# Gate and up in seven products: the seventh product's weight sum on VectorE, and products weight tile by weight tile with the high parts first

## The chip, the cores and the metric

The kernel runs on one core of a Trainium2 chip. The metric is device microseconds of one execution of the whole program: 1477.72 us is the median of three runs (1474.51 to 1479.86). Engines are named as in the profile: PE is TensorE (PEld its weight loads), DVE is VectorE, ACT is ScalarE, POOL is GpSimd, SP is SyncE, which here only issues DMAs.

## The reference, cut to what matters

A trunk of two layers over 512 tokens of 1024 features, in float32. Layer 0 mixes tokens by dilated window attention, layer 1 by gated linear attention; after each comes a feed-forward part:

```
def swiglu(h, w_gate_up, w_down):          # hidden width 2816
    g, u = jnp.split(h @ w_gate_up, 2, axis=-1)
    return (jax.nn.silu(g) * u) @ w_down

    h = h + mix.astype(h.dtype)
    h = h + swiglu(rms_norm(h, ffn_norm[i]), ffn_w_gate_up[i], ffn_w_down[i]).astype(h.dtype)
```

The change lies in the product `h @ w_gate_up` of both layers (512 x 1024 by 1024 x 5632).

## The kernel before, in words

**Split products.** Every float32 operand is split in two: ACT rounds it to the matmul's format (the high part, tiles `wh`), DVE subtracts that from the original (the low part, `wl`). A product is then three matmuls: high by high, high by low, low by high. `split` (lines 92 to 98) does it for weights: line 96 on ACT, line 97 on DVE. There are three buffers for `wh` and three for `wl`, each of 128 x 1024.

**Seven products for eight.** Gate and up are computed as a block product of 2 x 2 blocks: the tokens in two halves, the features in two halves, gate and up as the two column blocks. A scheme of Strassen's kind (Winograd's form) needs seven block products instead of eight, at the price of sums of blocks. The sums of the activations (`S1` to `S4`, made by `pair_sums` and `last_sums`, tiles `sh` and `sl`) are made once in a layer; the sums of the weights are made for every group of columns anew. The 2816 columns go in six groups `j`: five of 512, the last of 256. In each group the products come in the order first, second, fifth, sixth, third, seventh, fourth. One product is 24 matmuls of 128 x 512 (4 feature tiles, 2 token tiles, 3 terms), into two PSUM banks of 512 columns, one per token tile `i`. First, sixth, seventh and fourth add into the same pair of banks (`ppp`), and ACT copies the running sum out (line 379, tiles `g`) after the first, sixth and seventh; fifth and third share another pair (`ps`).

**The weights.** `forms` (line 236) is a generator: each step yields the split tiles of the next product. A 512-column block is two tiles of 128 x 1024 ("tile 1" and "tile 2" here; a tile holds two feature tiles). In groups 1 to 4 (`own` is false) the steps are:

- first: plain load of block 0 into `wA`, split
- second: plain load of block 1 into `wf`, split
- fifth: a DMA from POOL adds block 2 into `wA` in memory (line 251, `accum_op`), split; block 3 is loaded into `wB`
- sixth: DVE adds `wB` to `wA` (line 296), split
- third: a DMA adds block 1 into `wA`; `wB` as it stands is split
- seventh: a DMA adds block 2 into `wB`, split
- fourth: `wA` is split

Groups 0 and 5 (`own`) load a second copy of block 3 and make their sums ahead. `wf` has two buffers, `wB` two, `wA` four; `wf` also carries all plain weights of the other parts of the kernel.

**The order of the work.** Python issues the operations in program order; a scheduler with priorities (`high_priority` lets the steps of `forms` run ahead, `issue_after` holds something back) then writes one list per engine. Every engine works its list in order. What stands on DVE and ACT between the splits is the rest of the group: gates (lines 392, 393), the sums of lines 420, 421, 430 and 445, copies (379) and transposes (351). Finished columns go to memory by POOL's DMAs (`put`, line 359, held back until the last accumulating DMA of the group is issued) and come back transposed through SP's (`get`, line 365).

**The products.** `product` (lines 317 to 330) walks feature tile by feature tile; for each token tile it issues `xh` by `wh` (328), `xh` by `wl` (329) and `xl` by `wh` (330).

Of the kernel before, what the change touches and what calls it, by code (L numbers as in the profile page):

```python
# [21 lines left out]
P = 128  # L22
D = 1024
S = 512
KT = D // P
# [14 lines left out]
class Trunk:  # L40
# [195 lines left out]
    def forms(self, dram, own, ahead=0):  # L236
        nc = self.nc
        n = dram.shape[1]
        raw = {}
        started = ahead  # L240

        def load(block, tag, at=None, queue=nc.sync):
            raw[tag] = []
            for i in range(n):
                w = self.t(at or tag, (P, 1024))
                queue.dma_start(w, dram[block, i])
                raw[tag].append(w)

        def add(tag, block):
            for i in range(n):  # L250
                self.added = nc.gpsimd.dma_start(raw[tag][i], dram[block, i], accum_op=ALU.add)  # L251

        def ready(tag):
            return [self.split(w, (P, 1024), "wh", "wl") for w in raw[tag]]

        def sums(queue=nc.sync):
            load(0, "wA", queue=queue)
            add("wA", 2)
            load(3, "wB", queue=queue)
            raw["wC"] = raw["wB"]  # L260
            if not started:
                other_sum()

        def other_sum(queue=nc.sync):
            load(3, "wB", "wA", queue=queue)
            add("wB", 2)

        def first():
            if own and ahead:
                with self.tc.high_priority(offset=OUT):  # L270
                    sums(nc.gpsimd)
            if not own:
                load(0, "wA")
                return ready("wA")
            load(0, "wf")
            return ready("wf")

        def second():
            if own and not started:
                with self.tc.issue_after(self.added.ins):  # L280
                    sums()
            load(1, "wf")
            return ready("wf")

        def fifth():
            if not own:
                add("wA", 2)
                load(3, "wB")
                raw["wC"] = raw["wB"]
            elif started:  # L290
                other_sum(nc.gpsimd)
            return ready("wA")

        def sixth():
            for i in range(n):
                nc.vector.tensor_add(raw["wA"][i], raw["wA"][i], raw["wC"][i])
            return ready("wA")

        def third():
            add("wA", 1)  # L300
            return ready("wC")

        def seventh():
            if not own:
                add("wB", 2)
            return ready("wB")

        def fourth():
            return ready("wA")

        for step in (first, second, fifth, sixth, third, seventh, fourth):
            with self.tc.high_priority(offset=AHEAD + ahead):
                w = step()
            ahead = 0
            yield w

    def product(self, acc, x, w, width, start):
        mm = self.nc.tensor.matmul
        per = 1024 // width
        last = KT // 2 - 1  # L320
        for k in range(KT // 2):
            wh, wl = w[k // per]
            f = slice(k % per * width, (k % per + 1) * width)
            xh, xl = x[k]
            for i in range(2):
                tok = slice(i * P, (i + 1) * P)
                a = acc[i][:, 0:width]
                mm(a, lhsT=xh[:, tok], rhs=wh[:, f], start=start and k == 0, stop=False, skip_group_check=True)  # L328
                mm(a, lhsT=xh[:, tok], rhs=wl[:, f], start=False, stop=False, skip_group_check=True)  # L329
                self.multiplied = mm(a, lhsT=xl[:, tok], rhs=wh[:, f], start=False, stop=k == last, skip_group_check=True)  # L330

    def gate_up(self, layer, acts):
        nc = self.nc
# [915 lines left out]
```

## Time and profile before

| | |
|---|---|
| median of three runs | 1477.72 us (1474.51 to 1479.86) |
| span of the profiled execution, first to last instruction | 1475.3 us |
| time of that execution beside its span | not given by the page; the three runs are others |
| PE busy | 1449.8 us, 98% |
| DVE, ACT, POOL busy | 992.6, 756.1, 162.7 us |
| gate and up of layer 0, of layer 1 | about 565 to 787 us, 1128 to 1354 us |
| of these, groups 1 to 4 | about 604 to 762 us, 1167 to 1329 us |
| accumulating DMAs into `wB`, groups 1 to 4 | 8 in each layer |
| granted TensorE clock | 0.998 |

In a row of the timeline stand start, duration, engine, line, operation, and in brackets the idle time before it with what ended it. In the list of waits: engine, tile and line that waited, what it waited for, microseconds in total, how often, and the longest. In a grouped row: busy time and mean ns, then the idle time and its parts. A row of a window has busy time and count of PE, PEld, DVE, ACT and POOL, then the clock, the DMA engines' share and GB/s.

### The profile page before, as it was taken

The numbers are of one execution on the slowest core, as the hardware profiler recorded it, in microseconds if no ns is written. First come the engines' busy times: TensorE is split into PE (matmuls) and PEld (weight loads), VectorE is DVE, ScalarE is ACT, GpSimd is POOL, SyncE is SP. The second block draws the span as 40 slices with busy tenths as digits, with TensorE's granted clock in tenths as the row PEclk, the third lists the DMA queues.
The fourth block names the chain that finished last, engine by engine and source line by source line (L and its number), as shares of the span: only waits on it lengthen the run. The fifth ranks groups of instructions, "written<-read, shape, count | busy, mean of one in ns | idle before, by whom it ended". The sixth has DMA issues, their size and how long they took to land.

```text
span 1475.3 us, 20977 instructions
## 1 busy us (share of the span) xinstructions
PE 1449.8 (98%) x7742; PEld 1184.5 (80%) x7742; DVE 992.6 (67%) x1808; ACT 756.1 (51%) x1292; POOL 162.7 (11%) x272
## 2 busy tenths in 40 slices
PE   8999999999999999999999999999999999999998
PEld 6877878787778888877787887888888777778887
DVE  6586868778678669877676435756667876669322
ACT  6344444545566747655565324555745755556221
POOL 0001020101100021122230000000010122221000
PEclk9999999999999999999999999999999999999999
DMA  8644443454433365788887333212264788788431
GB/s 275 183 134 109 104 123 108 109 180 93 131 94 101 87 190 154 195 218 214 220 222 210 95 101 103 86 45 84 71 189 125 229 215 208 208 182 250 143 104 61
DMA packets 99831, 219.61 MB, mean 149 GB/s; under 512 B 15216, under 2 KB 42416, under 8 KB 99728
## 3 DMA queue, kind: packets, MB, share of 16 engines
q1 hardware_dynamic: 81072, 158.35, 34.5%
q0 software_dynamic: 18656, 59.91, 19.1%
q8 instruction: 61, 1.00, 0.3%
q14 instruction: 42, 0.34, 0.1%
HBM read 185.64 MB, written 19.99 MB: 139 GB/s over the span
## 4 chain that ended last, share of the span: by engine, by line
PE 66%; DVE 10%; issue 10%; DMA 7%; ACT 5%; POOL 1%; SPq 1%; DVEq 0%; POOLq 0%; ACTq 0%
PE ppp L110 9%; PE ppp L109 9%; PE ppp L108 9%; PE ppp L570 6%; PE ppp L571 6%; PE ppp L572 6%; PE ppp L329 3%; PE ppp L328 3%; PE ppp L330 3%; DVE wl L97 3%; DMA wA<-in_gate_up_last_dram 2%; DMA wB<-in_gate_up_dram 2%; PE po L701 2%; ACT wh L96 1%; PE ps L661 1%
## 5 line engine op out<-in xcount | busy, mean ns | idle before, releaser
L96 ACT ACTIVATE wh<-wf 128x1024 fp32r<-128x1024 f32 (+1 forms) x184 | 191.4, 1041 | 317.6 <-PE ppp L109 174.6
L97 DVE TENSOR_TENSOR wl<-wf,wh 128x1024 fp32r<-128x1024 f32 (+1 forms) x184 | 219.9, 1196 | 187.1 <-ACT wh L96 186.6
L570 PE MATMUL ppp<-wh,xs 128*128 128x512 f32 (+1 forms) x672 | 258.2, 385 | 7.2 <-ACT wh L96 5.7
L571 PE MATMUL ppp<-wl,xs 128*128 128x512 f32 (+1 forms) x672 | 257.3, 383 | 0.1
L572 PE MATMUL ppp<-wh,xs 128*128 128x512 f32 (+1 forms) x672 | 257.0, 383 | 0.0
L570 PEld LDWEIGHTS ppp<-wh,xs 128*128 128x128 f32 x672 | 126.8, 189 | 36.4 <-ACT wh L96 5.7
L572 PEld LDWEIGHTS ppp<-wh,xs 128*128 128x128 f32 x672 | 126.8, 189 | 25.6 <-issue 1.2
L571 PEld LDWEIGHTS ppp<-wl,xs 128*128 128x128 f32 x672 | 127.1, 189 | 24.8 <-DVE wl L97 0.9
L96 ACT ACTIVATE wh<-wA 128x1024 fp32r<-128x1024 f32 x88 | 93.2, 1059 | 73.4 <-PE ppp L330 27.3
L97 DVE TENSOR_TENSOR wl<-wA,wh 128x1024 fp32r<-128x1024 f32 x88 | 107.4, 1220 | 22.4 <-ACT wh L96 22.2
L329 PE MATMUL ppp<-wl,a 128*128 128x512 f32 (+1 forms) x288 | 108.1, 375 | 1.0 <-DVE wl L97 0.5
L328 PE MATMUL ppp<-wh,a 128*128 128x512 f32 (+1 forms) x288 | 108.4, 377 | 0.1
L108 PE MATMUL ppp<-xs,wh 128*128 128x512 f32 x272 | 106.5, 392 | 0.0
L109 PE MATMUL ppp<-xs,wh 128*128 128x512 f32 x272 | 106.5, 393 | 0.0
L110 PE MATMUL ppp<-xs,wl 128*128 128x512 f32 x272 | 106.0, 391 | 0.0
L330 PE MATMUL ppp<-wh,a 128*128 128x512 f32 (+1 forms) x288 | 105.5, 372 | 0.0
L97 DVE TENSOR_TENSOR wl<-wB,wh 128x1024 fp32r<-128x1024 f32 x38 | 46.5, 1223 | 78.2 <-ACT wh L96 78.2
L649 ACT ACTIVATE sm<-sm,st 128x160 f32<-128x160 f32 (+2 forms) x128 | 56.9, 446 | 43.5 <-DVE st L648 43.4
L329 PE MATMUL ppp<-wl,sh 128*128 128x512 f32 (+1 forms) x192 | 72.8, 379 | 4.6 <-DVE wl L97 4.4
L328 PE MATMUL ppp<-wh,sh 128*128 128x512 f32 (+1 forms) x192 | 71.9, 375 | 2.5 <-ACT g L379 1.8
L330 PE MATMUL ppp<-wh,sl 128*128 128x512 f32 (+1 forms) x192 | 71.6, 373 | 0.0
L251 POOL DMA_DIRECT2D wA<-in_gate_up_dram x44 | 38.5, 874 | 298.9 <-DVE wl L97 210.1
(319 smaller groups left out, 2949.0 us busy)
## 6 DMA issues: line engine op xcount, KB each, us to landing
wA<-in_gate_up_dram POOLq DMA_DIRECT2D x52, 512.0 KB, 6.1
wf<-in_down_dram SPq DMA_DIRECT2D x32, 512.0 KB, 3.7
wf<-in_gate_up_dram SPq DMA_DIRECT2D x24, 512.0 KB, 5.0
wf<-in_a_w_v_dram SPq DMA_DIRECT2D x20, 512.0 KB, 3.8
wB<-in_gate_up_dram POOLq DMA_DIRECT2D x20, 512.0 KB, 6.4
turned<-g POOLq DMA_DIRECT2D x80, 128.0 KB, 6.3
wf<-in_a_w_q_dram SPq DMA_DIRECT2D x16, 512.0 KB, 3.9
zq<-zs SPq DMA_DIRECT2D x128, 64.0 KB, 2.1
```

What stands on the lines that cost most here:

```text
L96: nc.scalar.activation(hi, src, AF.Copy)
L97: self.low = nc.vector.tensor_sub(lo, src, hi.bitcast(F32))
L108: mm(out, lhsT=wh, rhs=xh, start=start, stop=False)
L109: mm(out, lhsT=wh, rhs=xl, start=False, stop=False)
L110: self.multiplied = mm(out, lhsT=wl, rhs=xh, start=False, stop=stop)
L328: mm(a, lhsT=xh[:, tok], rhs=wh[:, f], start=start and k == 0, stop=False, skip_group_check=True)
L329: mm(a, lhsT=xh[:, tok], rhs=wl[:, f], start=False, stop=False, skip_group_check=True)
L330: self.multiplied = mm(a, lhsT=xl[:, tok], rhs=wh[:, f], start=False, stop=k == last, skip_group_check=True)
L570: mm(a, lhsT=xh, rhs=wh[:, f], start=k == 0, stop=False)
L571: mm(a, lhsT=xh, rhs=wl[:, f], start=False, stop=False)
L572: self.multiplied = mm(a, lhsT=xl, rhs=wh[:, f], start=False, stop=k == KT - 1)
L649: nc.scalar.activation(sm[:, w], sm[:, w], AF.Exp, bias=n, scale=-1.0, accum_out=l)
```

## The change

Two edits. In groups 1 to 4, block 2 is loaded a second time, plainly, into `wf` (issued by SP in the sixth step's place), and DVE adds `wB` (named `wC`) to it; the accumulating DMA into `wB` is gone. And `product` now goes weight tile by weight tile: first all matmuls that need the high part of the tile, then those that need its low part; in all but the last tile of a product for both token tiles together, in the last tile for token tile 0 completely and then for token tile 1.

```diff
         def sixth():
+            if not own:
+                load(2, "wf")
             for i in range(n):
                 nc.vector.tensor_add(raw["wA"][i], raw["wA"][i], raw["wC"][i])
             return ready("wA")
...
         def seventh():
-            if not own:
-                add("wB", 2)
-            return ready("wB")
+            if own:
+                return ready("wB")
+            for i in range(n):
+                nc.vector.tensor_add(raw["wf"][i], raw["wf"][i], raw["wC"][i])
+            return ready("wf")
...
-        for k in range(KT // 2):
-            wh, wl = w[k // per]
+        def high(i, k, wh):
             f = slice(k % per * width, (k % per + 1) * width)
-            xh, xl = x[k]
-            for i in range(2):
-                tok = slice(i * P, (i + 1) * P)
-                a = acc[i][:, 0:width]
-                mm(a, lhsT=xh[:, tok], rhs=wh[:, f], start=start and k == 0, stop=False, skip_group_check=True)
-                mm(a, lhsT=xh[:, tok], rhs=wl[:, f], start=False, stop=False, skip_group_check=True)
-                self.multiplied = mm(a, lhsT=xl[:, tok], rhs=wh[:, f], start=False, stop=k == last, skip_group_check=True)
+            for x_part, first in zip(x[k], (start and k == 0, False)):
+                mm(acc[i][:, 0:width], lhsT=x_part[:, i * P:(i + 1) * P], rhs=wh[:, f], start=first, stop=False,
+                   skip_group_check=True)
+
+        def low(i, k, wl):
+            f = slice(k % per * width, (k % per + 1) * width)
+            self.multiplied = mm(acc[i][:, 0:width], lhsT=x[k][0][:, i * P:(i + 1) * P], rhs=wl[:, f], start=False,
+                                 stop=k == last, skip_group_check=True)
+
+        for n, (wh, wl) in enumerate(w):
+            ks = range(n * per, n * per + per)
+            for group in ((0, 1),) if n < len(w) - 1 else ((0,), (1,)):
+                for i in group:
+                    for k in ks:
+                        high(i, k, wh)
+                for i in group:
+                    for k in ks:
+                        low(i, k, wl)
```

Lines from 331 on are 14 higher in the changed kernel; below, 309 is the new addition, 328 the matmuls on high parts and 333 those on low parts.

How the lists of the engines move is shown at three places. The first is DVE at the fifth and sixth products of group 2, layer 0; a row gives line, operation, output and inputs with buffer numbers. Before:

```order
L97 TENSOR_TENSOR wl_6639<-wf_6632,wh_6638 128x1024
L351 STREAM_TRANSPOSE g_6580<-g_6529 128x2x8x32
L97 TENSOR_TENSOR wl_6681<-wA_6587,wh_6680 128x1024
L296 TENSOR_TENSOR wA_6587<-wA_6587,wB_6676 128x1024
L97 TENSOR_TENSOR wl_6685<-wA_6589,wh_6684 128x1024
L392 TENSOR_TENSOR g_6625<-ppp_6628,g_6625 128x512
L296 TENSOR_TENSOR wA_6589<-wA_6589,wB_6678 128x1024
L97 TENSOR_TENSOR wl_6720<-wA_6587,wh_6719 128x1024
```

and now:

```order
L97 TENSOR_TENSOR wl_6643<-wf_6636,wh_6642 128x1024
L365 STREAM_TRANSPOSE g_6584<-g_6533 128x2x8x32
L309 TENSOR_TENSOR wf_6721<-wf_6721,wB_6680 128x1024
L97 TENSOR_TENSOR wl_6685<-wA_6591,wh_6684 128x1024
L298 TENSOR_TENSOR wA_6591<-wA_6591,wB_6680 128x1024
L97 TENSOR_TENSOR wl_6689<-wA_6593,wh_6688 128x1024
L309 TENSOR_TENSOR wf_6723<-wf_6723,wB_6682 128x1024
L298 TENSOR_TENSOR wA_6593<-wA_6593,wB_6682 128x1024
L97 TENSOR_TENSOR wl_6728<-wA_6591,wh_6727 128x1024
```

The additions for the seventh product stand three products ahead of it: the first ahead of the fifth product's first low part, the second ahead of the sixth product's sum. `wf_6721` is loaded into the buffer that the second product's split frees. (In group 1 both stand later, among the sixth product's low parts.)

The second place is PE where the seventh product of group 2 gives way to the fourth. Before, the fourth begins:

```order
L328 MATMUL ppp_6585<-wh_6833,a_5738 128x512
L329 MATMUL ppp_6585<-wl_6834,a_5738 128x512
L330 MATMUL ppp_6585<-wh_6833,a_5739 128x512
L328 MATMUL ppp_6585<-wh_6833,a_5789 128x512
L329 MATMUL ppp_6585<-wl_6834,a_5789 128x512
```

and now, with the last rows of the seventh (operands `sh`, `sl`) ahead of it:

```order
L328 MATMUL ppp_6590<-wh_6808,sl_5914 128x512
L333 MATMUL ppp_6590<-wl_6809,sh_5862 128x512
L333 MATMUL ppp_6590<-wl_6809,sh_5913 128x512
L328 MATMUL ppp_6589<-wh_6841,a_5738 128x512
L328 MATMUL ppp_6589<-wh_6841,a_5739 128x512
L328 MATMUL ppp_6589<-wh_6841,a_5789 128x512
L328 MATMUL ppp_6589<-wh_6841,a_5790 128x512
L333 MATMUL ppp_6589<-wl_6842,a_5738 128x512
L333 MATMUL ppp_6589<-wl_6842,a_5789 128x512
L328 MATMUL ppp_6590<-wh_6841,a_5738 128x512
```

The bank of token tile 0 (`ppp_6589`) gets its last matmul of the seventh product six matmuls before the end of it, where it was three, and the bank of token tile 1 is first written six matmuls into the fourth.

The third place is ACT in group 0 of layer 1, at the copies (line 379 before, 393 now) after the seventh product. Before:

```order
L379 ACTIVATE g_10714<-ppp_10438 128x512
L96 ACTIVATE wh_10776<-wA_10772 128x1024
L114 ACT_TABLE_LOAD
L114 ACTIVATE Rc_10627<-Rc_10626 128x4
L379 ACTIVATE g_10714<-ppp_10439 128x512
L115 ACT_TABLE_LOAD
L115 ACTIVATE Rc_10627<-Rc_10627 128x4
```

and now:

```order
L393 ACTIVATE g_10730<-ppp_10454 128x512
L114 ACT_TABLE_LOAD
L114 ACTIVATE Rc_10643<-Rc_10642 128x4
L96 ACTIVATE wh_10792<-wA_10788 128x1024
L115 ACT_TABLE_LOAD
L115 ACTIVATE Rc_10643<-Rc_10643 128x4
L393 ACTIVATE g_10730<-ppp_10455 128x512
```

The second copy moved behind the second table load. On POOL the two accumulating DMAs of each group are gone from between the third product's and the finished columns' writes; SP's list has the new loads behind the next group's first weights.

## The prediction

> **What bounds the kernel now.** The page's first part came first, then the waits of TensorE's weight loads, then single stretches in order of time.
>
> ```profile
> span 1475.3 us, 20977 instructions
> PE 1449.8 (98%) x7742; PEld 1184.5 (80%) x7742; DVE 992.6 (67%) x1808; ACT 756.1 (51%) x1292; POOL 162.7 (11%) x272
> ```
>
> TensorE (PE) is busy 98% of the span, so nothing outside its own stream matters unless PE is kept waiting. But ends of matmuls are modelled, so I read starts. The timeline at the seventh product of column group 3, layer 0:
>
> ```profile
> 709.26 0.39 PE L329 MATMUL ps<-wl,sh 128*128 128x512 f32 x1
> 709.49 0.39 PE L330 MATMUL ps<-wh,sl 128*128 128x512 f32 x1
> 709.77 0.51 PE L328 MATMUL ppp<-wh,sh 128*128 128x512 f32 x1
> 711.03 0.50 PE L329 MATMUL ppp<-wl,sh 128*128 128x512 f32 x1 [0.75 <-DVE wl L97]
> ```
>
> Undisturbed, starts are 0.227 us apart; a product of 24 takes 5.45. Here 711.03 - 709.77 = 1.26: one matmul with a low weight part lost 1.03 us. How much of this there is in the whole run stands in the waits of the weight loads (PEld; total us, times, longest). These rows belong to the gate and up products alone:
>
> ```profile
> PEld ppp L329 <- DVE wl L97: 13.9, 22, 1.1
> PEld ppp L328 <- ACT g L379: 6.9, 14, 1.5
> PEld ppp L328 <- ACT wh L96: 2.1, 4, 0.9
> ```
>
> Together 22.9 us in 40 waits. A load always idles a little (0.227 - 0.188 = 0.04 us, load time below), so 21.3 us is all that can be lost there, and the most that the change can win. By form:
>
> ```profile
> L329 PEld LDWEIGHTS ppp<-wl,a 128*128 128x128 f32 x288 | 54.2, 188 | 13.5 <-DVE wl L97 4.5
> L329 PEld LDWEIGHTS ppp<-wl,sh 128*128 128x128 f32 x192 | 36.1, 188 | 15.3 <-DVE wl L97 9.3
> ```
>
> 9.3 us stand before seventh products (sh), 4.5 in fourth and first ones (a), behind the same delay. Its origin in group 2:
>
> ```profile
> 662.57 0.89 POOL L251 DMA_DIRECT2D wB<-in_gate_up_dram  x1 [1.86 <-DVE wl L97]
> 668.83 1.06 ACT L96 ACTIVATE wh<-wB 128x1024 fp32r<-128x1024 f32 x1 [2.89 <-DMA wB<-in_gate_up_dram]
> 671.32 1.06 ACT L96 ACTIVATE wh<-wB 128x1024 fp32r<-128x1024 f32 x1 [1.43 <-DMA wB<-in_gate_up_dram]
> ```
>
> The accumulating DMA may start only when the third product's split has read wB; its 6.2 us are too long, and ScalarE (ACT) idles for it.
>
> **The change part by part.**
>
> *Sum on VectorE.* Both operands of the seventh sum are now loaded a product or more earlier, so the 6.2 us leave the path. VectorE (DVE) gets 16 additions of the size of
>
> ```profile
> L296 DVE TENSOR_TENSOR wA<-wA,wB 128x1024 f32<-128x1024 f32 x22 | 26.7, 1213 | 0.3
> 604.00:762.00 158.00, 156.22 (x674) 125.06 (x673) 112.43 (x126) 91.00 (x113) 40.61 (x57) 1.00 0.83 204
> ```
>
> 16 x 1.213 = 19.4 us. In groups 1 to 4 of layer 0 (second row) DVE is busy 112.4 of 158 us; with 8 more it is 122. As a load it is covered; what counts is where the additions stand. In groups 2 to 4 the first stands behind the second product's low parts, and its operand is loaded into the buffer that those have just freed:
>
> ```profile
> 646.05 3.32 SPq L246 DMA_DIRECT2D wf<-in_gate_up_dram  x2
> DMA to landing us min/median/max: 4.7/5.9/6.9
> 648.93 0.70 DVE L351 STREAM_TRANSPOSE g<-g 128x512 f32<-128x512 f32 x1
> 650.12 1.23 DVE L97 TENSOR_TENSOR wl<-wA,wh 128x1024 fp32r<-128x1024 f32 x1 [0.48 <-ACT wh L96]
> 654.26 0.39 PE L328 MATMUL ps<-wh,sh 128*128 128x512 f32 x1
> 659.71 0.39 PE L328 MATMUL ppp<-wh,sh 128*128 128x512 f32 x1
> ```
>
> (The second row is of these wf loads.) DVE reaches the addition at 649.6 and stands until 646.05 + 5.9 = 652.0, at worst 653.0. Behind it waits everything on DVE; PE feels the low parts of the fifth product (start 654.26) and the sixth (659.71). At worst: addition 654.2, fifth's first low part 655.4, sum and second low part 657.8, addition and sum 660.2, sixth's first low part 661.5, gate addition and second low part 663.4. They are wanted at 656.1, 657.9, 661.5 and 663.3, since the new order wants the first low part of a tile after 8 matmuls (1.82 us), of a last tile after 4 (0.91). So at 6.9 it just fits, at 5.9 with 1 us to spare; each us beyond 6.9 costs one us in six places (three groups, two layers). Below zero it cannot be: no earlier work depends on it. I take 0.2 each, 1.2 us; bounds 0 and, at the longest landing of a like load (9.4, quoted below), 6 x 2.5 = 15.
>
> The Trainium skill has a rule against this part (PSUM — Partial Sum Buffer, section Engine vs sequencer instructions): VectorE's queue is strictly first in, first out, so that ready splits cannot pass a waiting addition. By it the sum has the 1.2 us, up to 15; could they pass, 0. The trace shows nothing that speaks against it: DVE idles at 650.12 for its next instruction's operand.
>
> *Queues.* POOL loses 16 issues (0.89 us at 662.57) and its writes of the finished group move up by as much; nobody waits for them sooner. SP gets 16 plain loads. Behind them stand its loads for the next group: those of wf, that before followed the second product's low parts, now follow the seventh's, which leaves them the fourth and first products, 10.9 us, against at most 6.9. Cost 0; without that cover, what lands later than 10.9.
>
> *High parts first.* Low parts are wanted 8 or 4 matmuls into a tile, before after 1. That alone covers waits up to 1.59 or 0.68 us; with the DMA gone I remove 13.4 of the 13.9 us and all of the 2.1 for wh. The copies (6.9 us, 14): at the fourth product PE writes a bank that ACT is still copying.
>
> ```profile
> 676.32 0.39 PE L330 MATMUL ppp<-wh,sl 128*128 128x512 f32 x1
> 676.71 0.50 PE L328 MATMUL ppp<-wh,a 128*128 128x512 f32 x1
> 676.06 0.60 ACT L379 ACTIVATE g<-ppp 128x512 f32<-128x512 f32 x1 [0.98 <-PE ppp L330]
> 677.71 0.58 ACT L379 ACTIVATE g<-ppp 128x512 f32<-128x512 f32 x1
> ```
>
> The first copy starts 0.26 us before the last matmul, because its bank got its last one only 3 before the end. Now it is 6: the copy ends about 0.5 us before the product does. The second, behind a split of 1.06, ends 1.2 us after the product, and its bank is wanted after 6 matmuls (1.36). Where the 6.9 us lie: groups 1 to 4 (first row, the same in each layer), group 5 of layer 0 and of layer 1:
>
> ```profile
> PEld ppp L328 <- ACT g L379: 1.7, 4, 0.4
> PEld ppp L328 <- ACT g L379: 1.9, 2, 1.5
> PEld ppp L328 <- ACT g L379: 1.0, 2, 0.6
> ```
>
> Of 3.4 us in groups 1 to 4 I remove 2.8 and leave 0.6 for the narrow margin (1.36 against 1.2). In group 5 the second copy stands behind a split that waits for a DMA:
>
> ```profile
> 776.85 1.06 ACT L96 ACTIVATE wh<-wA 128x1024 fp32r<-128x1024 f32 x1 [2.10 <-DMA wA<-in_gate_up_last_dram]
> 777.81 0.37 ACT L379 ACTIVATE g<-ppp 128x256 f32<-128x256 f32 x1
> 778.23 0.19 PEld L328 LDWEIGHTS ppp<-wh,sh 128*128 128x128 f32 x1 [1.54 <-ACT g L379]
> ```
>
> PE now has 12 matmuls for the other bank instead of 3, each half as wide and so about 0.11 us: 1.0 us more cover. Of the two long waits, 1.5 and 0.6, I remove 1.0 and 0.6. What is left of the 6.9, in group 0, stays.
>
> *What gets worse.* (a) Layer 1, group 0: the second copy after the seventh product moves behind a second table load on ACT.
>
> ```profile
> 1161.73 1.06 ACT L96 ACTIVATE wh<-wA 128x1024 fp32r<-128x1024 f32 x1 [0.98 <-PE ppp L330]
> 1164.22 0.58 ACT L379 ACTIVATE g<-ppp 128x512 f32<-128x512 f32 x1
> 1164.82 1.28 ACT L115 ACT_TABLE_LOAD   x1
> 1164.85 0.19 PEld L328 LDWEIGHTS ppp<-wh,a 128*128 128x128 f32 x1 [0.36 <-ACT g L379]
> ```
>
> Between the first copy and the second, ACT had the split, a table load and a small step; now it has a second table load (1.28) and small step (0.2) as well, while the first table load may fill the 0.98 us that ACT idled. So the copy comes 0.5 to 1.5 us later, and PE waits for it already. I take 1.0. (b) Group 5's first weights can load only when group 4's seventh has freed wf, about 747.4, where before they had landed long ago; ACT wants them at 756.05, and the second copy stands behind them.
>
> ```profile
> 743.37 1.22 DVE L97 TENSOR_TENSOR wl<-wB,wh 128x1024 fp32r<-128x1024 f32 x1 [1.50 <-ACT wh L96]
> 756.05 1.06 ACT L96 ACTIVATE wh<-wf 128x1024 fp32r<-128x1024 f32 x1
> DMA to landing us min/median/max: 4.3/5.9/9.4
> ```
>
> (747.4 is the end of the first row, 744.6, and one tile of 2.72. The last row is of the wB loads; 9.4 is the one issued in this very stretch.) 8.65 us are there: 0 at the median, 0.8 at the longest. I take 0.8 in each layer, 1.6; bounds 0 and, if it lands at the chain's longest (11.4, below), 2 x 2.7.
>
> *Sum.* Removed 13.4 + 2.1 + 2.8 + 1.6 = 19.9 us, less 0.04 for each of some 35 waits: 18.5. Added 1.2 + 1.0 + 1.6 = 3.8. Net -14.7: span 1475.3 to 1460.6. The median of the three timings, 1477.7, lies 2.4 above the span (the page has no other time of that execution); carried over, **1463 us**.
>
> **The rivals.** *DVE stands too long (slower).* The plain load lands later than its place in DVE's queue allows. The gain without its 1.2 us is 15.9; it is used up at 15.9 / 6 = 2.7 us beyond 6.9, and the kernel is measurably slower (4.4 us) from 3.4 beyond, at 10.3. At the landing of the slowest accumulating DMA in the chain of waits,
>
> ```profile
> 745.97 11.36 DMA wA<-in_gate_up_last_dram
> ```
>
> 11.4 us, it costs 6 x 4.5 = 27: 1478 + 27 - 16 = 1489. For it: the loads share the DMA engines with accumulating DMAs and reads, 0.83 of their time in the window above. Against: the same buffers were reloaded at the same moment before and never took over 6.9; 16 accumulations leave. 0.05. Between 8.9 and 10.3 us gain and cost meet: *no change*, about 1478, 0.08. *Half of it*: the late wf in group 5 costs 2.7 a layer, 3.8 more in all, and the copies stay (2.8 + 1.6): 1463 + 3.8 + 4.4 = 1471; for it, ACT's order with a split between both copies. 0.13. *The left operand*: before, of three matmuls two neighbours had the same left operand xh; now none have. If the second load was saved so far and were not hidden now, the 672 loads of L329 would cost 672 x 0.188 = 126 us, 1604. Against: L329, which repeats L328's operand, has as many loads as matmuls and 188 ns each like the others, under the 227 of a matmul. 0.01. (The Trainium skill, TensorE: Matmul & The Clock Gate, section Step-by-step: what each phase is for, says that weights typically stay put across many matmuls and are loaded once for them; the trace's loads here are not of that kind.)
>
> **How the numbers follow.** The forecast has 0.73, by itself 1459 to 1468: lower if (a), (b) and the stall are 0 (1459), higher by some more than their sum again. Its range joined with the half gain up to 1472 leaves out the three last cases and a little below: **1458 to 1472**. A measurement can tell 0.3%, 4.4 us. Faster: 0.73 + 0.13 = 0.86; same 0.08; slower 0.06.
>
> **What would show it.** Right: the PEld waits of product() for wl fall below 1 us in groups 1 to 4 and no ACT wait for wB is left; starts stay 0.227 apart; DVE shows, once per group from 2 on, 2 to 3 us ended by a wf load and no PE wait behind it. (a): a PE wait for a copy near 1164 of 1 to 2 us; (b): ACT ended by a gate_up_last load ahead of the second copy in group 4. Wrong: PE waits for low parts in fifth and sixth products, or the 13.9 us turning up under another name.

## The result, and the profile after

The changed kernel takes 1463.06 us (median of five runs, 1462.55 to 1466.25) against 1477.72: 0.9912 of the time before, 95% interval 0.9897 to 0.9927. The medians are 14.7 us apart; the ratio stands for 13 us, the two profiled spans for 14.0. A second set of runs on another chip, made for the experiments below, gave 1464.04 and a ratio of 0.9922 (0.9906 to 0.9938). The profiled execution of the first set took 1463.06 us, with a span of 1461.3: what lies around the span is 1.8 us. The first part of its page:

```profile
span 1461.3 us, 21031 instructions
PE 1442.3 (99%) x7742; PEld 1186.6 (81%) x7742; DVE 1013.3 (69%) x1824; ACT 754.5 (52%) x1292; POOL 148.6 (10%) x256
```

DVE is 20.7 us busier for its 16 additions, POOL 14.1 us less busy, and the span is 14.0 us shorter. The rows of the waits of weight loads that are new or answer to those shown of before (total us, times, longest):

```profile
PEld ppp L328 <- ACT g L393: 5.6, 12, 1.3
PEld ppp L108 <- ACT g L481: 1.3, 2, 0.8
PEld pt L218 <- issue: 0.6, 1, 0.6
PEld pt L218 <- DVE acc L156: 0.5, 1, 0.5
```

The two rows on `wl` and `wh` (13.9 and 2.1 us) have no successor: in the products nothing waits for a split any more. The waits for copies fell only from 6.9 to 5.6; eight of them stand in groups 1 to 4 (2.4 us) and cost the starts 0.1 to 0.2 us each, but for 0.6 in group 4 of layer 1. And there are waits that were 0.2 us or nothing before: for the split columns of the down product (L481) and before the small matmuls into `pt` (L218). By form, the loads of low parts (busy us, mean ns, idle us, and what ended most of it):

```profile
L333 PEld LDWEIGHTS ppp<-wl,a 128*128 128x128 f32 x288 | 51.7, 188 | 9.4
L333 PEld LDWEIGHTS ppp<-wl,sh 128*128 128x128 f32 x192 | 34.5, 188 | 6.2
```

No releaser stands behind the idle time: 9.4 / 288 and 6.2 / 192 are 0.03 us per load, no more than the 0.227 - 0.188 us that stand between undisturbed loads. Groups 1 to 4, from the first matmul of group 1 to the first of group 5 (layers 0 and 1 after, then layer 1 before):

```profile
604.70:757.60 152.90, 152.90 (x674) 125.84 (x674) 123.65 (x134) 89.38 (x113) 33.36 (x49) 1.00 0.76 212
1162.80:1316.00 153.20, 152.93 (x673) 125.80 (x672) 124.36 (x135) 90.60 (x114) 33.68 (x49) 1.00 0.78 213
1167.30:1329.40 162.10, 157.57 (x673) 124.79 (x672) 113.42 (x126) 91.74 (x114) 40.58 (x57) 1.00 0.80 198
```

Undisturbed, 672 starts 0.227 us apart take 152.5 us, so that of 5.5 and 9.6 us lost in them before, 0.4 and 0.7 are left. DVE is busy 124 us of 153 where the prediction had 122 of 158. The whole span, cut at the first matmuls of groups 0, 1 and 5 in each layer:

| stretch | before, us | after, us | change |
|---|---|---|---|
| to group 0 of layer 0 | 564.8 | 565.1 | +0.3 |
| group 0, layer 0 | 39.2 | 39.6 | +0.4 |
| groups 1 to 4, layer 0 | 158.0 | 152.9 | -5.1 |
| group 5 and down of layer 0, mixing of layer 1 | 366.0 | 364.7 | -1.3 |
| group 0, layer 1 | 39.3 | 40.5 | +1.2 |
| groups 1 to 4, layer 1 | 162.1 | 153.2 | -8.9 |
| group 5 and down of layer 1, to the end | 145.9 | 145.3 | -0.6 |

Together -14.0. That is what groups 1 to 4 won; the changes of the other stretches cancel.

### The profile page after: what moved, and what is told of

It is laid out like the page before. It is cut to its first block, busy times and chain, and to the rows that moved or that the text cites. A ratio compares the mean times of both kernels' runs of the same rounds, so it can differ in the third digit from the quotient of the medians.

```text
span 1461.3 us, 21031 instructions
## 1 busy us (share of the span) xinstructions
PE 1442.3 (99%) x7742; PEld 1186.6 (81%) x7742; DVE 1013.3 (69%) x1824; ACT 754.5 (52%) x1292; POOL 148.6 (10%) x256
## 4 chain that ended last, share of the span: by engine, by line
PE 80%; DVE 10%; ACT 4%; DMA 4%; issue 2%; SPq 0%; DVEq 0%; ACTq 0%
PE ppp L328 11%; PE ppp L109 9%; PE ppp L108 9%; PE ppp L110 9%; PE ppp L584 7%; PE ppp L585 7%; PE ppp L586 7%; PE ppp L333 5%; PE ps L328 4%; DVE wl L97 2%; PE ps L333 2%; PE po L715 2%; ACT sm L663 1%; PE ps L675 1%; DMA h_dram<-h 1%
## 5 line engine op out<-in xcount | busy, mean ns | idle before, releaser
L97 DVE TENSOR_TENSOR wl<-wf,wh 128x1024 fp32r<-128x1024 f32 (+1 forms) x200 | 239.4, 1198 | 204.8 <-ACT wh L96 204.2
L96 ACT ACTIVATE wh<-wf 128x1024 fp32r<-128x1024 f32 (+1 forms) x200 | 208.0, 1041 | 321.5 <-PE ppp L109 173.2
L328 PE MATMUL ppp<-wh,a 128*128 128x512 f32 (+1 forms) x576 | 140.2, 374 | 2.2 <-ACT g L393 2.2
L328 PEld LDWEIGHTS ppp<-wh,a 128*128 128x128 f32 x576 | 101.7, 188 | 24.0 <-ACT g L393 5.6
L110 PE MATMUL ppp<-xs,wl 128*128 128x512 f32 x272 | 106.0, 391 | 0.0
L333 PE MATMUL ppp<-wl,a 128*128 128x512 f32 (+1 forms) x288 | 78.4, 371 | 0.0
L328 PE MATMUL ps<-wh,sh 128*128 128x512 f32 (+1 forms) x192 | 70.3, 371 | 0.0
L328 PE MATMUL ps<-wh,sl 128*128 128x512 f32 (+1 forms) x192 | 70.3, 371 | 0.0
```

The costliest lines, as they stand in the source:

```text
L96: nc.scalar.activation(hi, src, AF.Copy)
L97: self.low = nc.vector.tensor_sub(lo, src, hi.bitcast(F32))
L110: self.multiplied = mm(out, lhsT=wl, rhs=xh, start=False, stop=stop)
L328: mm(acc[i][:, 0:width], lhsT=x_part[:, i * P:(i + 1) * P], rhs=wh[:, f], start=first, stop=False, skip_group_check=True)
L333: self.multiplied = mm(acc[i][:, 0:width], lhsT=x[k][0][:, i * P:(i + 1) * P], rhs=wl[:, f], start=False, stop=k == last, skip_group_check ...
```

## The experiments

Times are medians; each ratio is against runs of the kernel before on the same chip (1475.98, 1475.0 and 1477.35 us in the three sets). Line numbers are those of each kernel.

### The two halves of the change

The first set held the changed kernel again, its two halves apart, and the changed kernel with another order in the last weight tile.

> The changed kernel itself, on the same chip as the next three, so that they can be compared with it. Both theories: 1463 us, 14 to 15 below the kernel before.

Measured: 1464.04 us, 0.9922 (0.9906 to 0.9938), as expected within 1 us.

**Only the order of the matmuls.** The edit, against the changed kernel:

```diff
-            if not own:
-                load(2, "wf")
...
-            if own:
-                return ready("wB")
-            for i in range(n):
-                nc.vector.tensor_add(raw["wf"][i], raw["wf"][i], raw["wC"][i])
-            return ready("wf")
+            if not own:
+                add("wB", 2)
+            return ready("wB")
```

> Only the new order of the matmuls; the seventh sum is again made by the accumulating DMA. Theory A (two covers for one wait): the low part was late by 1.1 us at most, and the new order wants it 1.59 or 0.68 us later than the old one, so the order alone removes nearly all waits on low parts and the copies' waits too; waits on high parts of seventh products (2.1 us) and 0 to 2 us in second weight tiles stay: 1465 to 1467 us. Theory B (division of labour, as the prediction adds it up: the sum on VectorE removes the waits on low parts, the order those on copies): ScalarE and VectorE still get the DMA's result 6 us late, 10 to 12 us of waits stay, and only the 3 to 4 us of the copies go: 1473 to 1475 us.

Measured: 1483.32 us, 1.0055 (1.0042 to 1.0069). Both theories fell: the order alone makes the kernel slower than before. Its waits, and the same stretches (groups 1 to 4 of each layer, before 158.0 and 162.1 us):

```profile
PEld ppp L324 <- ACT wh L96: 15.1, 9, 2.9
PEld ppp L324 <- ACT g L389: 8.2, 11, 1.4
PEld ppp L329 <- DVE wl L97: 4.1, 10, 0.5
605.00:768.60 163.60, 156.48 (x673) 126.41 (x672) 112.74 (x124) 87.94 (x113) 40.16 (x57) 0.99 0.80 197
1176.20:1336.10 159.90, 154.86 (x673) 125.28 (x672) 112.31 (x124) 90.08 (x114) 40.53 (x57) 1.00 0.80 200
```

The waits for low parts did shrink (13.9 to 4.1). But the seventh product now waits for its *high* part, up to 2.9 us, and for that the new order has no cover: a high part is the first thing that a tile needs. (By the profiled spans this kernel is 8.6 us slower than the one before. Groups 1 to 4 have 3.5 of that, 5.7 more in layer 0 and 2.2 less in layer 1; group 0 has 1.6; 3.0 come from group 5 on, where the waits for copies grew from 2.9 to 6.0 us; why they grew stays open.) The DMA that adds into `wB` had become later and longer. POOL's issues around it in group 2, layer 0, in this kernel and then before:

```profile
661.06 0.85 POOL L251 DMA_DIRECT2D wA<-in_gate_up_dram  x1 [16.84 <-DVE wl L97]
662.79 0.86 POOL L251 DMA_DIRECT2D wA<-in_gate_up_dram  x1 [0.88 <-DVE wl L97]
664.22 0.89 POOL L251 DMA_DIRECT2D wB<-in_gate_up_dram  x1 [0.57 <-DVE wl L97]
665.66 0.87 POOL L251 DMA_DIRECT2D wB<-in_gate_up_dram  x1 [0.55 <-DVE wl L97]
```

```profile
657.65 0.85 POOL L251 DMA_DIRECT2D wA<-in_gate_up_dram  x1 [12.85 <-DVE wl L97]
659.85 0.86 POOL L251 DMA_DIRECT2D wA<-in_gate_up_dram  x1 [1.34 <-DVE wl L97]
662.57 0.89 POOL L251 DMA_DIRECT2D wB<-in_gate_up_dram  x1 [1.86 <-DVE wl L97]
665.29 0.87 POOL L251 DMA_DIRECT2D wB<-in_gate_up_dram  x1 [1.84 <-DVE wl L97]
```

Four accumulating DMAs of 512 KB within 4.6 us instead of 7.6, the two into `wB` 1.4 us apart instead of 2.7. (The delay begins earlier: ScalarE's split for the sixth product starts 15.3 us into the group instead of 11.1, behind a landing of 11.4 us instead of 8.1 in the fifth step, and behind a gate that the scheduler has put ahead of it on ScalarE's list.) The issues of DMAs with their median time to landing, groups 1 to 4 of layer 0, before, in this kernel, and in the run that comes next:

```profile
wB<-in_gate_up_dram POOLq DMA_DIRECT2D x8, 512.0 KB, 6.2
```

```profile
wB<-in_gate_up_dram POOLq DMA_DIRECT2D x8, 512.0 KB, 7.9
```

```profile
wB<-in_gate_up_dram POOLq DMA_DIRECT2D x8, 512.0 KB, 5.5
```

**The same with fewer adds**, to tell the DMAs' own time from the engines' lists: in groups 1 to 4 the third step's accumulating DMA is left out.

```diff
-            add("wA", 1)
+            if own:
+                add("wA", 1)
             return ready("wC")
```

> The order alone (as in the run that was slower than the kernel before, 1483 us), with the third step's accumulating DMA left out in groups 1 to 4, so that the fourth product's weights lack block 1; ScalarE's list is the same. There the two DMAs of the third step and the two of the seventh stood within 4.6 us, against 7.6 us before, and the seventh's landed after 7.9 us against 6.2. Theory A (the bunched DMAs slow each other): the seventh's land after 6.0 to 6.4 us, most of the 15.1 us of waits for high parts go: 1468 to 1475 us. Theory B (the lists of ScalarE and VectorE issue the DMA late, its landing is not at fault): landing stays near 7.9, 1481 to 1484 us.

Measured: 1466.55 us, 0.9948 (0.9931 to 0.9965), a little faster than Theory A had it. Groups 1 to 4 take 152.8 and 153.0 us, and one wait for a split, of 0.4 us, is left in them. ScalarE's and VectorE's lists are the same in both, so the lists alone don't make the seventh product wait; with the third step's adds they do. Two effects go together here: without those adds the seventh's land sooner (5.5 us against 7.9), and in group 2 of layer 0 they are issued sooner (19.5 us into the group instead of 21.1; 19.2 before).

The run of the order alone parts the two. In its group 2 of layer 1 the first add into `wB` is issued 18.7 us into the group, sooner than before (19.2), and lands after 8.9 us instead of 6.6; the first matmul of the seventh product still starts 1.65 us late. There the landing alone is enough. In group 1 of each layer the four adds stand 7.4 and 7.3 us apart, those into `wB` land after 6.0 to 6.3 us, and the seventh product loses nothing.

**Only the sum on VectorE**, with the old order of the matmuls (the first two hunks of the change without the third).

> Only the plain load and the sum on VectorE; the matmuls keep the old order, in which a low part is wanted one matmul after its high part. Theories A and B: the waits before seventh and fourth products for low and high parts go (11 to 12 us by the starts of the matmuls), the waits for copies (about 3 us in groups 1 to 4) stay, nothing changes in group 5: 1466 to 1468 us. A third theory (the sum only moves the delay): VectorE's stand of 2 to 3 us at the new addition now meets low parts wanted 0.3 to 0.6 us after they are made, so that fifth and sixth products wait in its place: 1470 to 1474 us.

Measured: 1466.11 us, 0.9935 (0.9920 to 0.9950). Its waits in the products (L332 to L334 are the three matmuls of the old order, L383 the copy):

```profile
PEld ppp L332 <- ACT g L383: 6.5, 15, 0.9
PEld ppp L333 <- DVE wl L97: 1.6, 3, 1.0
PEld ps L333 <- DVE wl L97: 0.6, 1, 0.6
```

The sum alone takes 13.9 us of waits for low parts down to 2.2, and leaves those for copies (6.9) as they were. Of the 2.2 us for low parts, 1.0 stands at the first product of layer 1's group 1, where it stood before too; the other 1.2, at the fifth and sixth product of one group, are all that there is of the third theory. So by the medians of this set the sum alone brings 9.9 us, the order on top of it 2.1 (which the intervals don't tell from nothing), and the order without it costs 7.3. The two halves do not add; the order's gain needs the sum.

**The token tiles together**, to test how the new order helps the copies:

```diff
-            for group in ((0, 1),) if n < len(w) - 1 else ((0,), (1,)):
+            for group in ((0, 1),):
```

> The changed kernel, but in a product's last weight tile too the token tiles go together: four high pairs, then all low parts, so that the first bank gets its last matmul 3 from the end instead of 7. If the early end of the first bank is what took the waits for copies away, they come back with 0.35 to 0.5 us at each of 8 fourth products and some in groups 0 and 5: 1466 to 1468 us. If the copies were freed by the rest of the change (ScalarE no longer waiting for the DMA), it stays at 1463.

Measured: 1465.14 us, 0.9927 (0.9913 to 0.9941): 1.1 us over the changed kernel on the same chip, less than the intervals can tell, and under the 3 to 5 expected. By the starts, from group 0 to the end, it is 1.3 us longer than that kernel's run. The edit did more than was meant. Behind the seventh product the starts lose 0.4 us in each of the eight groups, 3.2 us in all, as much as expected, but not for the copies. In group 2 of layer 0:

```profile
675.99 1.06 ACT L96 ACTIVATE wh<-wA 128x1024 fp32r<-128x1024 f32 x1 [1.66 <-PE ppp L328]
676.95 1.06 ACT L393 ACTIVATE g<-ppp 128x512 f32<-128x512 f32 x2
677.10 2.81 PE L328 MATMUL ppp<-wh,a 128*128 128x512 f32 x11 [0.24 <-ACT wh L96]
```

A weight tile has 8 matmuls with its high part, and here stand 11: the scheduler has put three of the next group's first product ahead of the fourth product (5 are left at that product's own place). PE waits for the split of their weights, which ends at 677.05, and the three cover the first copy. On the other side, of what the changed kernel loses later in its fourth products, 0.4 and 0.8 us in group 4 and 0.7 and 0.9 in group 5, only 0.1 each is left, since ScalarE now makes the two copies one after the other. So the kernel does almost as well without the early end of one bank; what that early end is worth by itself the run doesn't show.

### How much VectorE may stand

Two kernels make the operand of the new addition late. The first addition is held ahead of the fifth product's splits on VectorE's list, and a load of 64 KB (columns 0 to 127) or 512 KB goes into the same buffer first; the second load has to wait until the first has landed.

```diff
+            if not own:
+                raw["wf"] = []
+                for i in range(n):
+                    w = self.t("wf", (P, 1024))
+                    nc.sync.dma_start(w[:, 0:128], dram[1, i, :, 0:128])
+                    nc.sync.dma_start(w, dram[2, i])
+                    raw["wf"].append(w)
+                first_sum = nc.vector.tensor_add(raw["wf"][0], raw["wf"][0], raw["wC"][0])
+                with self.tc.issue_after(first_sum.ins):
+                    return ready("wA")
             return ready("wA")
```

> The changed kernel with the seventh sum's operand made late: ahead of each of the two loads a load of 64 KB goes into the same buffer, so that the load proper is issued some 2.3 us later (a load of 64 KB takes about 2.1 us to land), and the first addition is held in its place in VectorE's list, ahead of the fifth product's low parts. In the changed kernel the first low part of the fifth product is ready 2.2 us before it is wanted (group 2, layer 0), and this is the smallest room but one. Theory A (room, then one for one in six to eight places): 0.1 to 0.3 us beyond the room, 1463 to 1466 us. Theory B (no room: the stand of 2 to 3 us is just what the change can bear, as the prediction had it with 1 us to spare): 1.3 us in six places, 1471 us. Theory C (the additions are not on TensorE's path at all): 1463, and the next kernel too.

> The same, with a load of 512 KB ahead of each load, so that the load proper comes some 5.4 us later (the median landing of these loads). Theory A: 5.4 - 2.1 = 3.3 us in six places, and about as much in group 1 of each layer, where the first addition is now held ahead of the low parts as well: 20 to 27 us, 1483 to 1490 us. Theory B: 4.4 us in six to eight places, 1490 to 1498. Theory C: 1463 to 1466 us.

Measured: 1478.27 us, 1.0026 (1.0014 to 1.0039), with runs from 1475.0 to 1483.1; and 1483.50 us, 1.0060 (1.0043 to 1.0077). The first is 12 us above what Theory A expected, because the delay was larger than meant: in group 2 of layer 0 the load of 64 KB took 5.8 us to land, not 2.1. Against the delay that the trace shows, Theory A holds closely. The first addition and the load of the fifth product's first low part in group 2, layer 0, of the first kernel and of the second:

```profile
655.10 1.23 DVE L299 TENSOR_TENSOR wf<-wf,wB 128x1024 f32<-128x1024 f32 x1 [6.20 <-DMA wf<-in_gate_up_dram]
657.51 0.77 PEld L340 LDWEIGHTS ps<-wl,sh 128*128 128x128 f32 x4 [1.64 <-DVE wl L97]
```

```profile
657.23 1.22 DVE L299 TENSOR_TENSOR wf<-wf,wB 128x1024 f32<-128x1024 f32 x1 [7.39 <-DMA wf<-in_gate_up_dram]
659.64 0.77 PEld L340 LDWEIGHTS ps<-wl,sh 128*128 128x128 f32 x4 [2.82 <-DVE wl L97]
```

Counted from the first matmul of the second product, the addition starts 6.22 and 7.40 us later, and the fifth product's starts lose 1.54 and 2.68: both times 4.7 less. In the sixteen groups of the two kernels the difference is 4.68 to 4.72 in all that lost anything, but for one (7.02 and 3.94); the two that started at 3.73 and 4.59 lost nothing there. So there is a room, and beyond it the loss is one for one, with 0.2 us more at the sixth product in all but two of the sixteen. In the changed kernel the first addition of groups 2 to 4 starts 1.3 to 2.6 us after the second product does (in the second set 1.0 to 2.7), so 2 us of room are left. The kernel with the 64 KB load lost another 1.8 us at the fourth product of group 4 in each layer, where group 5's first weights came late (ScalarE waited 2.1 us for them in layer 0).

### What is left in groups 0 and 5

The last kernels go after the waits that the change left or made. An attempt to spare the two table loads of layer 1's group 0:

```diff
             self.sums = [None] * (KT // 2)
+            if layer == 1:
+                self.nc.scalar.preload_act_table_set("natural_log_exp_and_others")
             out_projection()
```

> The changed kernel with ScalarE's table of logarithm and exponential loaded once before layer 1's output projection, so that the two table loads between the first and the second copy of group 0 (1.28 us each) go. Theory A (the copy stands behind the table loads, as the prediction's step (a) has it): the wait of 1.3 us before the fourth product falls to about 0.3 as in layer 0, about 0.9 us less: 1462 us, and the rows show it even where the time can't. Theory B (the copy waits for something else, or the gain returns as a wait for the token norm at group 1's start): the wait stays or moves.

Measured: 1463.54 us, 0.9927 (0.9912 to 0.9943). It tells nothing of its question: no load of that line stands in the trace, and both old ones are where they were, with a wait of 1.2 us behind them.

**Group 0 mended**: the load now stands behind the first copy of group 0, and the small matmuls into `pt` behind the seventh product.

```diff
             g1 = copy(b1)
+            if j == 0 and layer == 1:
+                with self.tc.issue_after(self.copied.ins):
+                    nc.scalar.preload_act_table_set("natural_log_exp_and_others")
...
+            if j == 0:
+                with self.tc.issue_after(self.multiplied.ins):
+                    R = self.token_norm()
+                gates()
+                third_sums()
```

(`third_sums` is lines 432 to 435 as a function, called here in group 0 and in its old place otherwise.)

> The changed kernel with group 0 mended: the sums over tokens (the small matmuls into pt) stand behind the seventh product instead of inside it, and in layer 1 the table of logarithm and exponential is loaded once, early in group 0 (the earlier attempt left no such load in the trace). Theory A (each wait is what the rows say): 0.4 us in each layer before those matmuls and 0.9 us at the second copy of layer 1 go, 1.7 us less: 1462 us. Theory B (a floor): the token norm comes later by about 1 us, its result is wanted by the activations that free the banks for group 1, and the first product of group 1 waits in their place: 1463 to 1465 us.

Measured: 1462.50 us, 0.9904 (0.9890 to 0.9917). In the trace group 0 loses nothing before the small matmuls and 0.14 us at the fourth product in each layer, where the second set's run of the changed kernel lost 0.24 and 1.12; from its first matmul to that of group 1 the group is 0.6 and 1.4 us shorter. ScalarE around the two copies in layer 1, in the changed kernel and now:

```profile
1155.65 1.28 ACT L114 ACT_TABLE_LOAD   x1
1157.05 1.04 ACT L96 ACTIVATE wh<-wA 128x1024 fp32r<-128x1024 f32 x1
1158.12 1.28 ACT L115 ACT_TABLE_LOAD   x1
1159.52 0.58 ACT L393 ACTIVATE g<-ppp 128x512 f32<-128x512 f32 x1
```

```profile
1155.17 1.06 ACT L96 ACTIVATE wh<-wA 128x1024 fp32r<-128x1024 f32 x1 [0.31 <-PE ppp L328]
1156.13 0.58 ACT L393 ACTIVATE g<-ppp 128x512 f32<-128x512 f32 x1
1156.61 0.20 ACT L114 ACTIVATE Rc<-Rc 128x4 f32<-128x4 f32 x1
```

Theory A holds, and no floor shows: group 1's first product loses nothing in either layer, in spite of the token norm's later start.

**Group 5's second copy first**, by holding back the splits of finished columns:

```diff
-        for k in range(len(pairs), NH):
-            pairs.append(self.halves(acts[k], k))
+        with self.tc.issue_after(self.copied.ins):
+            pairs += [self.halves(acts[k], k) for k in range(len(pairs), NH)]
```

> The changed kernel with ScalarE's splits of the finished columns for the down product held back until the last copy of group 5, so that the second copy comes 0.9 us earlier (two small splits of 0.6 us stand ahead of it). Theory A (what group 5 wins is given back): the wait of 0.9 us before the fourth product of group 5 goes in both layers, and the first down product then waits as much longer for the last finished columns, whose load from memory is issued late: 1463 to 1464 us, as the changed kernel. Theory B (the gain stays): 1.8 us less, 1462 us.

Measured: 1464.76 us, 0.9915 (0.9902 to 0.9927), the time of the changed kernel. The wait before group 5's fourth product went (0.7 and 0.9 to 0.1 us by the starts), and the down product's wait for the last columns, 1.3 us in two in the changed kernel (1.6 in the second set), grew:

```profile
PEld ppp L108 <- ACT g L481: 2.5, 2, 1.3
```

By the starts group 5 won 1.5 us more than in the second set's run of the changed kernel, and the down product gave back 1.0 more, 20 us later. That is Theory A for two thirds. **With the last two columns loaded through POOL's queue** (`get(nc.gpsimd)` in the last loop, lines 471 and 472):

> The same, and the loads of the last two finished columns of each layer go through POOL's queue, where they no longer stand behind a weight load of SP's that waits for a free buffer (in the changed kernel issued at 792.6 us, though the columns had been written by 789.2). Theory A: now group 5's 0.9 us stay won and the down product's wait of 0.7 to 0.9 us goes too: 3.3 us less, 1460 to 1461 us. Theory B (the loads' place doesn't matter): as the run before.

Measured: 1462.25 us, 0.9900 (0.9887 to 0.9914), 2.5 us under the run before. The first of these loads is now issued 32.6 and 32.0 us after group 5's first matmul (layers 0 and 1) instead of 34.6 and 34.8; of the down product's 2.5 us 0.2 are left in this row, and 0.6 us wait in layer 1 for VectorE's half of the same split. From group 5 to the end of the down product the starts are 1.3 us shorter than in the run before; the rest of the 2.5 lies elsewhere and is within the intervals. It came out 1 to 2 us above Theory A's figure.

**All together:**

> All of these together. Theory A (they add): 1463.5 - 3.3 - 1.7 = 1458.5 us. Theory B (the gains are swallowed by waits behind them): 1461 to 1463 us.

Measured: 1460.18 us, 0.9887 (0.9874 to 0.9901): 17.2 us under the kernel before, 2.3 and 2.1 under each of the two part mends, and the fastest of all that were run. Theory A had 1458.5. By the starts, group 0 is 2.0 us shorter in both layers together than in the second set's run of the changed kernel, and the stretch from group 5 through the down product 2.4: 4.4 of the 5.0 expected, so the gains add. In its trace the waits of the products are one row, and more than half of it lies in group 4 (0.9 and 1.5 us by the starts, for group 5's late first weights):

```profile
PEld ppp L328 <- ACT g L393: 4.2, 8, 1.7
```

## Why the prediction was right, and where not

The forecast was 1463 us, and the time is 1463.06; the span came to 1461.3 against 1460.6. The mechanism was as described, but several terms were off and made up for each other; that the total came out so close is luck.

**What the waits were worth.** The step "13.4 + 2.1 + 2.8 in groups 1 to 4, less 0.04 for each" is mis-sized. The list has 7.3 and 12.1 us of waits in 15 and 19 places there, and the starts of the matmuls lost 5.5 and 9.6. The difference is 0.13 us a wait, not 0.04: undisturbed, a load starts one matmul ahead of its own (the load for the matmul at 713.66 started at 713.43), and a short wait spends that lead first. A load that waited 0.57 us, and the starts around it:

```profile
714.20 0.19 PEld L329 LDWEIGHTS ppp<-wl,sh 128*128 128x128 f32 x1 [0.57 <-DVE wl L97]
713.66 0.39 PE L328 MATMUL ppp<-wh,sh 128*128 128x512 f32 x1
714.20 0.50 PE L329 MATMUL ppp<-wl,sh 128*128 128x512 f32 x1
714.53 0.40 PE L330 MATMUL ppp<-wh,sl 128*128 128x512 f32 x1
```

From 713.66 to 714.53 two intervals took 0.87 where 0.45 is undisturbed: 0.42 lost, not 0.53. So 15.1 us were there to be won in groups 1 to 4, and 1.1 are left, where the prediction's terms come to a gain of 17.0. The copies are one such term: with the sum alone the starts lose 0.31 us around the fourth product of groups 1 to 3, in the changed kernel 0.12, so about 1.5 us were won there in eight groups, not 2.8.

**VectorE's stand (1.2 us).** The stand is there as forecast, 12.5 us in six places, the longest 2.6, and costs nothing. Group 2 of layer 0, the addition, the fifth product's two splits behind it, and the matmuls that want them:

```profile
651.02 1.23 DVE L309 TENSOR_TENSOR wf<-wf,wB 128x1024 f32<-128x1024 f32 x1 [2.62 <-DMA wf<-in_gate_up_dram]
652.16 1.22 DVE L97 TENSOR_TENSOR wl<-wA,wh 128x1024 fp32r<-128x1024 f32 x1
654.56 1.22 DVE L97 TENSOR_TENSOR wl<-wA,wh 128x1024 fp32r<-128x1024 f32 x1
655.63 1.07 PE L333 MATMUL ps<-wl,sh 128*128 128x512 f32 x4
657.45 0.62 PE L333 MATMUL ps<-wl,sh 128*128 128x512 f32 x2
```

Ready at 653.4 and 655.8, wanted at 655.6 and 657.5: 2.2 and 1.7 us of room, where the prediction had 1. That each us beyond the room costs one us was right, as the late loads showed (4.7 us after the second product's start, then one for one). The rival that takes this mechanism as its place, 1489 us, was priced about rightly too: with the additions of group 2 3.6 and 4.8 us later than in the changed kernel, the whole came to 1478 and 1484, though the room was 2 us and not 1, and losses in group 1 and for group 5's weights came on top. By the Trainium skill's rule (PSUM — Partial Sum Buffer, section Engine vs sequencer instructions: VectorE's queue is strict FIFO) nothing passes a waiting addition; the traces agree, since in 6.20 us of standing no split went ahead, though ScalarE's half of the next split was done at 649.85, 5.25 us before the addition began.

**(b), late weights of group 5 (1.6 us in both layers).** Right in place, and in size on the average, but it varies. In the profiled run the starts lost 0.16 and 0.56 us at the fourth product of group 4; over seven kernels with the same groups the layers' means are 0.5 and 0.9 us, with 0.1 and 1.8 as the ends. The run with 1.8 shows the chain as it was described, ScalarE waiting for the load ahead of the second copy:

```profile
1309.89 1.06 ACT L96 ACTIVATE wh<-wf 128x1024 fp32r<-128x1024 f32 x1 [1.96 <-DMA wf<-in_gate_up_last_dram]
1310.86 0.58 ACT L393 ACTIVATE g<-ppp 128x512 f32<-128x512 f32 x1
```

The landing was wrong: the loads are issued 23.9 us into group 4, near the forecast 24.4 (747.4 in the old kernel's time), but take 8.4 to 9.1 us in the profiled run, and 7.9 to 10.2 over the seven, not 5.9.

**(a), the table loads (1.0 us).** Right: the copy starts at 1159.52 behind the second table load (the rows are above), PE waits 1.3 us where it was 0.4, and the starts lose 0.85 us more. With the loads gone the wait went too.

**Group 5's copies (1.6 us won).** Wrong in part. The waits of 1.5 and 0.6 us at the seventh product are gone, but each layer has a new one of 0.8 at the fourth: there the second copy stands behind two splits of finished columns and one of down weights, of which the prediction said nothing.

```profile
774.77 1.14 ACT L481 ACTIVATE sl<-xs 128x512 fp32r<-128x512 f32 x2
775.81 1.05 ACT L96 ACTIVATE wh<-wf 128x1024 fp32r<-128x1024 f32 x1
776.76 0.37 ACT L393 ACTIVATE g<-ppp 128x256 f32<-128x256 f32 x1
```

In its stead the two waits of 1.0 us of the first down matmuls (L110), which stood inside group 5 before, went, since these matmuls now stand behind the product. Net, group 5 won 2.9 us in both layers by the starts, and the down product gave back 1.0 of them at the last columns: 1.9, near the forecast by luck, since it came by other ways.

**What was missing.** The small matmuls into `pt` now find their operand not ready and cost 0.4 us a layer. And the down product's wait: nobody asked what PE would meet 20 us after it had become earlier. The 2.4 us between span and median were 1.8 in the profiled run of the changed kernel.

In sum, groups 1 to 4: 17.0 forecast and 2.8 charged against it (the stand and (b)) gave 14.2, and 14.0 came, since only 0.5 of the charges was due in this run and the gain was 2.5 smaller. The rivals with no change (0.08) and half the gain (0.13) did not come, nor did that of the left operand (the starts are 0.227 us apart as before); the forecast's own range, 1459 to 1468, held. That the half of the change which looks harmless, the order, would alone have made the kernel slower by 7 us was nowhere in the prediction: it took the DMA's 6.2 us as given.

## What to carry to other kernels

Price a stall by the starts of the matmuls, not by the idle time of the loads; here the list of waits overstated 15 us by 4. Of a change with two halves ask what each does to the DMAs: here the new order alone, with the lists that the scheduler made for it, brought four adds closer together, and what was covered came back as a wait for the one thing without cover. When a wait has gone, look for the next point where the engine meets data from memory, in the next stage too: 1.0 us of the 1.5 won by a mend in group 5 was lost again 20 us on, until the loads were issued earlier.

## What the runs showed of the hardware

The time of a DMA depended strongly on its neighbours. The accumulating DMA of 512 KB landed after 5.5 us (median of groups 1 to 4 in layer 0) when two of its kind stood by themselves, 6.2 when there were four (within 7.6 us in group 2), and 7.9 with four closer together (4.6 us in group 2). By the Trainium skill (DMA: Bandwidth & Descriptors, section Issuing engines are not separate DMA queues), DMAs of all issuing engines run on the same DMA engines and interleave. Whether POOL's adds slow SP's plain loads is not shown here: those into `wf` took 5.0 us before and 6.6 with the order alone in layer 0, but 6.1 and 5.5 in layer 1. Size mattered less than place: a load of 64 KB took 5.8 us to land when it was issued among others, and the 512 KB load issued as it landed took 3.4. A load of ScalarE's table took 1.28 us in each case.
